# When stores, weight loads and head values are asked for, and how far the filling may run, in a fused attention and recurrence block

## The chip, the cores and the metric

The kernel runs on one core of one Trainium2 chip. The metric is the device time of one execution in microseconds (us), as the median of several runs. The profile is one further execution, taken by the hardware profiler. In it TensorE is PE, its weight loads PEld, VectorE DVE, ScalarE ACT, GpSimd POOL and SyncE SP.

## The reference

One residual block over 1024 rows of width 1024, in float32. Two branches work on the same normalised input: stick-breaking attention with 8 heads of 64, and a gated linear recurrence (HGRN2) with 4 heads of 128. Each branch is projected, gated, and the sum is projected again; a feed-forward part follows.

```python
xn = rmsnorm(x, norm1_g)
q_sb, k_sb, v_sb, f_raw, i_hg, q_hg, g_hg, gate_sb, gate_hg = split(xn @ w_in)
o_sb = merge(stick_breaking_attention(q_sb, k_sb, v_sb))       # 8 heads
o_hg = merge(rmsnorm(hgrn2_chunkwise(silu(q_hg), (1 - lb) * sigmoid(-f_raw), i_hg, log_f)))
o_hg = o_hg * silu(g_hg)                                        # 4 heads
merged = sigmoid(gate_sb + b) * (o_sb @ w_o_sb) + sigmoid(gate_hg + b) * (o_hg @ w_o_hg)
h = x + merged @ w_out
return h + square(relu(rmsnorm(h) @ w_ff1)) @ w_ff2
```

## The kernel before

Every float32 product is made of three products of parts: each operand is split into a high part (a CAST on ACT) and a low part (a subtraction on DVE), `hi_lo` with its two lines 154 and 159, and `three` issues high by high, low by high and high by low on PE (line 131). A product of 128 rows by 512 columns is one such matmul. Some products are formed with fewer multiplications from sums of blocks (seven products for a 2 by 2 arrangement), which is why sums of inputs and sums of weights are needed.

The program is one stream of code. A scheduler then places the instructions on each engine by their dependences, costs and due times; the order of the code sets due times, not places. DMAs are issued from three queues, each in order: SP (loads), POOL (stores of intermediate tiles and some loads from DRAM) and ACT (a few stores).

The parts that matter here, in order of time:

- **Input sums (early_sums, about 59 to 72 us).** From the transposed input four sums are formed for each of two column blocks (forms 6, 5, 7, 3), split into `efh` and `efl`, and each of the 16 tiles (512 KB each) is stored on POOL's queue to `form..` for the gates' projections, which load them again (`gsh`, `gsl`) at about 557 to 598 us. `vrows` are stores of the attention's values on the same queue, released by ACT's copies `v<-pjv` (line 663).
- **The pairs (ProjPair, about 70 to 165 us).** Four pairs of column blocks of the input projection, each with seven products m1 to m7. `wp1a` and `wp1b` are the raw weights of the second pair (two loads of 256 KB each, on SP's queue, in pieces of 64 columns); `whia` and `wloa` are the split parts of the first. `pu` is a copy on ACT of a product out of the result banks (`ppX`), which frees the bank for the next product: m7 waits for the copy of m6.
- **The attention heads (about 165 to 510 us).** Items of one head and one block of rows: scores `z`, `rm` (a scan on DVE, line 982), transposes `pw`, weights `wTh`, `wTl`, and products `po`. Between them stand filling products, `pga`, `pgq` (the raw gates, RawUnit; `wga0r` are the weights of the first, `wga0t` a split sum of them) and `pji` (values of the recurrence, with weights `wi0`).
- **The recurrence (about 510 to 637 us).** Heads h = 0 to 3, each with levels of decayed scores `sl` (k, q and pp updated on DVE in between), state sums `pk` and `pkv` (the latter with the head's values `v`, loaded from `irows` on POOL's queue by `i_load`), outputs `pho`, their norm (`hon`, ACT and POOL and DVE) and a transpose `pot`. The loop runs over h = 0 to 4; in turn h it works on the levels of head h and the tail of head h - 1. Filling products stand between, at most up to a job that is set for each turn: `j_raw[cb]` is the raw gate of column block cb (`pga`, `pgq`), `j_sb[n]` the n-th block of the attention's output projection (`pys`, with weights `wo00` to `wo03`).
- **The gates (from 637 us).** `gX` is the first of their products; its weights are `wg0`, split into `whig`, `wlog`, `tgh`, `tgl`, and `woh`, `wol`; the next ones are `wg4`.

The loop of the recurrence reads:

```python
FILL = (3.6, 3.1, 2.65, 2.45, 2.8)
for h in range(NHG + 1):
    lev = hg_levels(h) if h < NHG else iter(())
    tail = hg_tail(h - 1) if h > 0 else iter(())
    upto = (j_hg[2], j_hg[3], j_raw[6], j_sb[1], j_sb[3])[h]
    if h > 0:
        i_load(h - 1)
    ...
                owed += FILL[h]
                st.advance(int(owed), upto)
```

Of the kernel before, what the change touches and what calls it, by code (L numbers as in the profile page):

```python
# [9 lines left out]
F32 = mybir.dt.float32  # L10
# [9 lines left out]
P = 128  # L20
# [8 lines left out]
NHG = 4  # L29
# [10 lines left out]
def kernel(  # L40
# [19 lines left out]
    nc = tc.nc  # L60
# [11 lines left out]
    wpool = ctx.enter_context(tc.tile_pool(name="wts", bufs=2))  # L72
    psum = ctx.enter_context(tc.tile_pool(name="psum", bufs=8, space=PSUM))

    def slot(name, dt=F32):
        return spool.tile([P, 1024], dt, tag="s", name=name)
# [11 lines left out]
    def dram(name, shape):  # L88
        return scratch.tile(shape, F32, tag=name, name=name)
# [4 lines left out]
    def bank(name):  # L94
        return psum.tile([P, 512], F32, tag="p", name=name)
# [66 lines left out]
    def hi_lo(h, l, src):  # L162
        hi_copy(h, src)
        return lo_sub(l, src, h)
# [518 lines left out]
    def v_split(h):  # L683
        r = vraw.pop(h)
        nc.vector.tensor_tensor(out=r[:, 0:512], in0=r[:, 512:], in1=r[:, 0:512], op=ALU.subtract)
        vt[h] = slot(f"V{h}", F32R)
        V = vt[h].rearrange("p (t s d) -> p t s d", s=2, d=DHS)
        hi_lo(V[:, :, 0, :], V[:, :, 1, :], r[:, 0:512].rearrange("p (t d) -> p t d", d=DHS))
# [90 lines left out]
    def early_whole(half_, engine):  # L779
        for kp in range(KT // 2):  # L780
            h, l = (t.bitcast(F32) for t in xn.t[half_, kp])
            early[half_, kp // 2, kp % 2] = t = slot(f"xw{half_}{kp}")
            engine.tensor_tensor(out=t, in0=h, in1=l, op=ALU.add)

    early_forms = {}
    formd = {(m, kp): dram(f"form{m}{kp}", [P, 2, T]) for m in (3, 5, 6, 7) for kp in range(2)}

    def early_sums():
        def form(m, kp, src):
            early_forms[m, kp] = tuple(slot(f"ef{n}{m}{kp}", F32R) for n in "hl")  # L790
            hi_lo(*early_forms[m, kp], src)
            for i, t in enumerate(early_forms[m, kp]):
                nc.gpsimd.dma_start(formd[m, kp][:, i, :], t.bitcast(F32))

        w = early

        def tt(out, a, b, op):
            nc.vector.tensor_tensor(out=out, in0=a, in1=b, op=op)

        for kp in range(2):  # L800
            tt(w[1, 1, kp], w[1, 0, kp], w[1, 1, kp], ALU.add)
            tt(w[1, 0, kp], w[0, 0, kp], w[1, 0, kp], ALU.subtract)
            tt(w[0, 0, kp], w[1, 1, kp], w[0, 0, kp], ALU.subtract)
            form(6, kp, w[0, 0, kp])
        for kp in range(2):
            form(5, kp, w[1, 1, kp])
        for kp in range(2):
            form(7, kp, w[1, 0, kp])
        for kp in range(2):
            tt(w[0, 1, kp], w[0, 1, kp], w[0, 0, kp], ALU.subtract)  # L810
            form(3, kp, w[0, 1, kp])

    class ProjPair:
# [6 lines left out]
        def load(self):  # L820
            self.raw = []
            for n, parts in (("a", self.pa), ("b", self.pb)):
                r = wpool.tile([P, 1024], F32, tag="raw", name=f"wp{self.i}{n}")
                c = 0
                for c0, w in parts:
                    load(
                        r.rearrange("p (k c) -> p k c", k=KT)[:, :, c : c + w],
                        W_IN[:, c0 : c0 + w].rearrange("(k p) c -> p k c", p=P),
                    )
                    c += w  # L830
                self.raw.append(r)
# [106 lines left out]
    def scores(h, qb):  # L938
        open_block("main")
        nk = (qb + 1) * P  # L940
        QH, QL, KS = qk[h]
        rm = slot_n(f"rm{h}_{qb}", nk)
        step = 320 if nk == 640 else 512
        for s0 in range(0, nk, step):
            m = min(nk - s0, step)
            n = max(m, 256)
            z = bank(f"z{h}_{qb}_{s0}")
            for i, Q in enumerate((QH, QL)):
                matmul(
                    z[:, :n],  # L950
                    Q[:, qb * P : (qb + 1) * P],
                    KS[:, s0 : s0 + n],
                    start=i == 0,
                    stop=i == 1,
                )
            nc.scalar.activation(rm[:, s0 : s0 + m], z[:, :m], AF.Sigmoid, scale=-0.125)  # L956
        zs[h, qb] = rm
# [14 lines left out]
    def weights(h, qb):  # L972

        nk = (qb + 1) * P
        rm = zs[h, qb]
        cut = qb == NT - 1
        parts = ((512, nk), (0, 512)) if cut else ((0, nk),)
        for i, (a, b) in enumerate(parts):  # L980
            rr = rm[:, a:b][:, ::-1]
            sc = nc.vector.tensor_tensor_scan(  # L982
                out=rr,
                data0=rr,
                data1=bits[:, 1024 - nk + a : 1024 - nk + b][:, ::-1],
                initial=rm[:, b : b + 1] if i else 0.0,
                op0=ALU.mult,
                op1=ALU.max,
            )
            if i == 1 or (qb == 5 and h in (2,)):  # L990
                after(sc, turn_lo[0])
# [134 lines left out]
    def i_load(h):  # L1126
        hg[h, "v"] = slot(f"v{h}")
        nc.gpsimd.dma_start(
            chunks(hg[h, "v"]),
            irows[:, h * P : (h + 1) * P].rearrange("(t p) c -> p t c", p=P),  # L1130
        )
# [9 lines left out]
    j_hg = {}  # L1141
# [327 lines left out]
    raw_units = [RawUnit(cb) for cb in range(KT)]  # L1469

    def raw_job(cb):
        u = raw_units[cb]

        def steps_of(ps, wt, w0, half_, k0, start):
            wh, wl = u.hl[wt]
            for k in range(4):
                c = (w0 + k) * P
                xh, xl = xn.mov(k0 + k, half_)
                three(
                    ps, wh[:, c : c + P], wl[:, c : c + P], xh, xl, start and k == 0, k == 3, True  # L1480
                )
                if k % 2 == 1:
                    yield

        def body():
            p1, p14, g1 = (half(f"{n}_{cb}") for n in ("p1", "p14", "g1"))
            ps, p4 = bank(f"pga{cb}"), bank(f"pgq{cb}")
            if cb >= 6:
                load_g1(cb - 6)
            if cb >= 4:  # L1490
                osb[cb - 4] = slot(f"osr{cb - 4}")
                load(osb[cb - 4], osd[cb - 4])
            yield from steps_of(ps, 0, 0, 0, 0, True)
            hi_behind[0] = nc.scalar.copy(p1, ps)
            nc.scalar.dma_start(pd[cb][:, 0, :], p1)
            if cb == 0:
                u.split_t()
            st.prefetch()
            hi_behind[0] = None
            yield from steps_of(p4, 1, 0, 1, 4, True)  # L1500
            add(p14, p1, p4)
            nc.gpsimd.dma_start(pd[cb][:, 1, :], p14)
            yield from steps_of(ps, 0, 4, 0, 4, False)
            nc.scalar.activation(g1, ps, AF.Sigmoid, bias=gate_bias(0, cb))
            nc.scalar.dma_start(gd[cb], g1)
            if cb >= 4:
                a_sb.put(cb - 4, osb[cb - 4])

        return st.add([u], body)
# [55 lines left out]
    j_raw = [raw_job(0)]  # L1565
# [11 lines left out]
    j_sb = [sb_job(cp) for cp in range(4)]  # L1577
# [740 lines left out]
    proj = [ProjPair(i, *blocks[2 * i : 2 * i + 2]) for i in range(4)]  # L2318
# [3 lines left out]
    proj[0].split_plain()  # L2322
    proj[0].m1()
    proj[0].split_sums()
    for o, n in zip(proj, proj[1:] + [None]):
        o.m2()
        if n:
            n.load()
        else:
            scores(*items[0])  # L2330
        o.m6()
        if not n:
            weights(*items[0])
        o.m5()
        if n:
            n.split_plain()
        else:
            scores(*items[1])
        if o is proj[-2]:
            qk_load(0)  # L2340
            v_load(0)
        o.m7()
        if n:
            n.m1()
            n.split_sums()
        o.m4()
        o.m3()
    v_split(0)

    n_fill = 4 * 7 + 2 * 9 + 2 * 17  # L2350
# [4 lines left out]
    for i, it in enumerate(items):  # L2355
# [19 lines left out]
        r = turn(*it, between)  # L2375
# [14 lines left out]
    for h in range(NHG + 1):  # L2390
        lev = hg_levels(h) if h < NHG else iter(())
        tail = hg_tail(h - 1) if h > 0 else iter(())
        upto = (j_hg[2], j_hg[3], j_raw[6], j_sb[1], j_sb[3])[h]
        if h > 0:
            i_load(h - 1)
        if h == 1:
            hg[0, "g"] = slot("g0")
            nc.gpsimd.dma_start(hg[0, "g"], gsd)
        going = True
        while going:  # L2400
            going = False
            for g in (lev, tail):
                if next(g, StopIteration) is not StopIteration:
                    going = True
                    owed += FILL[h]
                    st.advance(int(owed), upto)
                    owed -= int(owed)
        if h + 1 < NHG:
            st.finish(j_hg[h + 1])
        if h > 1:  # L2410
            a_hg.put(h - 2, ohg[h - 2], hg_level[0])
# [102 lines left out]
```

## Time and profile before

| | us |
|---|---|
| runs before: median (lowest to highest of 3) | 1481.63 (1476.57 to 1483.03) |
| the profiled execution | 1478.12 |
| its span, first to last instruction | 1476.4 |
| TensorE busy in it | 1434.8 (97%) |
| DVE, ACT, POOL busy | 1085.1 (73%), 648.9 (44%), 175.8 (12%) |
| mean granted TensorE clock | 0.990 |

The span is 1.7 us shorter than the profiled execution's own time, which is 3.5 us under the median of the runs. A wait is read from the profile as the idle time of an engine ahead of an instruction, with what ended it in brackets. The granted clock (PEclk) is 1.00 at full speed.

### The profile page before, as it was taken

The page shows a single profiled execution, that of the slowest core. Times are in us where ns is not written, and L with a number is a line of the kernel's source. Part 1 is how long each engine was busy: PE and PEld are TensorE (multiplying, and loading weights), DVE is VectorE, ACT ScalarE, POOL GpSimd, SP SyncE. Part 2 cuts the span into 40 slices and gives each one's busy share as a digit, 9 for nine tenths or more (in the row PEclk, how much of TensorE's full clock was granted, in tenths as well). Part 3 has the DMA queues.
Part 4 walks back from the last instruction along what each step waited for, and adds up shares of the span by engine and source line. Part 5 has one row for each costly group of instructions (what it writes and reads, how often), then busy time and mean ns, then how long its engine had stood idle before and what let it go on. Part 6 is the DMA issues. An engine that isn't in the chain of part 4 may idle for free. (4 is left out here: it accounts for less than half of the span.)

```text
span 1476.4 us, 19878 instructions
## 1 busy us (share of the span) xinstructions
PE 1434.8 (97%) x7422; PEld 1220.5 (83%) x7422; DVE 1085.1 (73%) x1526; ACT 648.9 (44%) x1056; POOL 175.8 (12%) x333
## 2 busy tenths in 40 slices
PE   8979899999999999799998999999999999999998
PEld 8968799988888888688887888888888888888886
DVE  6946688798976888568875899676766666768765
ACT  6433566566322333333333575444444443433433
POOL 3322222322000011101110110000000000000032
PEclk9999999999999999999999999999999999999999
DMA  6576765986211267655468533444444985676835
GB/s 222 183 222 206 228 175 161 216 178 152 72 44 44 67 212 277 216 167 175 143 197 262 199 127 129 157 157 156 154 145 151 341 294 199 228 270 235 290 102 187
DMA packets 170857, 270.82 MB, mean 183 GB/s; under 512 B 27612, under 2 KB 95752, under 8 KB 170760
## 3 DMA queue, kind: packets, MB, share of 16 engines
q1 hardware_dynamic: 149272, 206.36, 42.6%
q0 software_dynamic: 17744, 56.64, 12.3%
q10 hardware_dynamic: 3744, 6.56, 1.2%
q8 instruction: 58, 0.95, 0.3%
q14 instruction: 39, 0.32, 0.1%
HBM read 192.44 MB, written 85.46 MB: 188 GB/s over the span
## 5 line engine op out<-in xcount | busy, mean ns | idle before, releaser
L154 ACT CAST whid<-w 128x1024 fp32r<-128x1024 f32 x30 | 31.6, 1053 | 153.6 <-PE pm L131 86.0
L982 DVE TENSOR_TENSOR_SCAN rm<-rm,bits 128x512 f32<-128x512 f32 (+6 forms) x72 | 87.4, 1222 | 8.9 <-ACT rm L956 8.4
L131 PE MATMUL pm<-wlod,sh 128*128 128x512 f32 x240 | 93.5, 389 | 0.0
L131 PE MATMUL pm<-whid,sh 128*128 128x512 f32 x240 | 93.4, 389 | 0.0
L131 PE MATMUL pm<-whid,sl 128*128 128x512 f32 x240 | 93.4, 389 | 0.0
L131 PE MATMUL pm<-tl,sh 128*128 128x512 f32 (+1 forms) x210 | 81.3, 387 | 0.0
L131 PE MATMUL pm<-th,sl 128*128 128x512 f32 (+1 forms) x210 | 81.3, 387 | 0.0
L131 PE MATMUL pm<-th,sh 128*128 128x512 f32 (+1 forms) x210 | 81.3, 387 | 0.0
L159 DVE TENSOR_TENSOR wlod<-w,whid 128x1024 fp32r<-128x1024 f32 x30 | 36.7, 1223 | 59.0 <-ACT whid L154 58.7
L2123 POOL TENSOR_SCALAR fss<-fss 128x1 f32<-128x1 f32 x8 | 4.5, 562 | 562.1 <-ACT fsc L2118 561.6
L159 DVE TENSOR_TENSOR sl<-sa,sh 128x1024 fp32r<-128x1024 f32 x56 | 68.2, 1218 | 1.0 <-ACT sh L154 1.0
L1030 ACT ACTIVATE wTh<-pw,minus_one 128x512 fp32r<-128x512 f32 (+2 forms) x96 | 53.4, 583 | 33.1 <-PE pw L134 29.1
L1036 DVE SCALAR_TENSOR_TENSOR wTl<-pw,wTh 128x512 fp32r<-128x512 f32 (+2 forms) x96 | 50.4, 548 | 16.3 <-ACT wTh L1030 15.6
L154 ACT CAST sh<-sa 128x1024 fp32r<-128x1024 f32 x56 | 57.2, 1045 | 7.0 <-DMA sa<-ad 7.0
L131 PEld LDWEIGHTS pm<-wlod,sh 128*128 128x128 f32 x240 | 45.0, 187 | 9.9 <-DVE wlod L159 0.6
L131 PEld LDWEIGHTS pm<-whid,sl 128*128 128x128 f32 x240 | 45.1, 188 | 9.4
L131 PEld LDWEIGHTS pm<-whid,sh 128*128 128x128 f32 x240 | 45.1, 188 | 9.2
L131 PE MATMUL pX<-sql,t1h 128*128 128x512 f32 x128 | 50.0, 391 | 0.1
L131 PE MATMUL pX<-sqh,t1l 128*128 128x512 f32 x128 | 49.8, 389 | 0.0
L131 PE MATMUL pX<-sqh,t1h 128*128 128x512 f32 x128 | 49.8, 389 | 0.0
L131 PEld LDWEIGHTS pm<-tl,sh 128*128 128x128 f32 x210 | 39.5, 188 | 8.2
L131 PEld LDWEIGHTS pm<-th,sh 128*128 128x128 f32 x210 | 39.4, 188 | 8.0
(962 smaller groups left out, 4573.5 us busy)
## 6 DMA issues: line engine op xcount, KB each, us to landing
w<-in_w_ff_dram SPq DMA_DIRECT2D x72, 512.0 KB, 5.4
sa<-ad SPq DMA_DIRECT2D x56, 512.0 KB, 6.5
ad<-a SPq DMA_DIRECT2D x32, 256.0 KB, 4.4
ad<-s SPq DMA_DIRECT2D x16, 512.0 KB, 5.6
tw<-in_w_out_dram POOLq DMA_DIRECT2D x24, 256.0 KB, 6.0
x<-in_x_dram SPq DMA_DIRECT2D x8, 512.0 KB, 8.4
qkh<-qkh POOLq DMA_DIRECT2D x16, 256.0 KB, 3.9
qkl<-qkl POOLq DMA_DIRECT2D x16, 256.0 KB, 4.7
```

The lines of the kernel that those rows point to most:

```text
L131: return pe(nc.tensor.matmul(*a, **k))
L154: hi_last[0] = after(in_turn("act", nc.scalar.copy(dst, src)), hi_behind[0])
L159: nc.vector.tensor_tensor(out=dst, in0=src, in1=hi.bitcast(F32), op=ALU.subtract),
L982: sc = nc.vector.tensor_tensor_scan(out=rr, data0=rr, data1=bits[:, 1024 - nk + a : 1024 - nk + b][:, ::-1], initial=rm[:, b : b + 1] if i ...
L1030: nc.scalar.activation(th[:, 0:n, qs], src, AF.Identity, bias=minus_one),
L1036: nc.vector.scalar_tensor_tensor(out=tl[:, 0:n, qs], in0=src, scalar=-1.0, in1=th[:, 0:n, qs].bitcast(F32), op0=ALU.add, op1=ALU.subtract,),
L2123: nc.gpsimd.tensor_scalar(out=ssq, in0=ssq, scalar1=1.0 / D, scalar2=EPS, op0=ALU.mult, op1=ALU.add)
```

## The change

It has four edits, in code order:

1. `early_sums` no longer issues the 16 stores itself. It puts them on a list (`kept`), and `keep(n)` issues the next n of them on POOL's queue. Over the last three pairs `spread` asks for one store at each of seven places; what is left is issued after the pairs.
2. The raw weights of the second pair go into slots of their own and not into the two buffers that the pairs share; they are loaded ahead of the pairs' loop, and each turn of the loop then loads the weights of the pair after the next.
3. The first raw gate's weights are loaded ahead of `weights(*items[0])`, and split (with the split sum `wga0t`) in the last pair, ahead of m4. Until now `wga0t` was split inside the gate's own job.
4. In the recurrence `i_load(h)` stands in turn h (was: `i_load(h - 1)`), and the filling may run to `j_raw[7]` in turn 2 and `j_sb[2]` in turn 3 (was `j_raw[6]`, `j_sb[1]`).

```diff
+    kept = deque()
+
+    def keep(n):
+        for _ in range(min(n, len(kept))):
+            dst, t = kept.popleft()
+            nc.gpsimd.dma_start(dst, t.bitcast(F32))
...
-            for i, t in enumerate(early_forms[m, kp]):
-                nc.gpsimd.dma_start(formd[m, kp][:, i, :], t.bitcast(F32))
+            kept.extend((formd[m, kp][:, i, :], t) for i, t in enumerate(early_forms[m, kp]))
...
-                r = wpool.tile([P, 1024], F32, tag="raw", name=f"wp{self.i}{n}")
+                if self.i == 1:
+                    r = slot(f"wp{self.i}{n}")
+                else:
+                    r = wpool.tile([P, 1024], F32, tag="raw", name=f"wp{self.i}{n}")
...
-            if cb == 0:
-                u.split_t()
...
-    for o, n in zip(proj, proj[1:] + [None]):
+    proj[1].load()
+    for o, n, m in zip(proj, proj[1:] + [None], proj[2:] + [None] * 2):
+        def spread():
+            if o is not proj[0]:
+                keep(1)
+
         o.m2()
-        if n:
-            n.load()
-        else:
+        if m:
+            m.load()
+        elif not n:
             scores(*items[0])
+        spread()
         o.m6()
         if not n:
+            raw_units[0].load()
             weights(*items[0])
+        spread()
...
         o.m7()
+        spread()
         if n:
             n.m1()
             n.split_sums()
+        else:
+            raw_units[0].split()
+            raw_units[0].split_t()
+        spread()
         o.m4()
+        spread()
         o.m3()
+    keep(len(kept))
     v_split(0)
...
-        upto = (j_hg[2], j_hg[3], j_raw[6], j_sb[1], j_sb[3])[h]
-        if h > 0:
-            i_load(h - 1)
+        upto = (j_hg[2], j_hg[3], j_raw[7], j_sb[2], j_sb[3])[h]
+        if h < NHG:
+            i_load(h)
```

What this does to the order on the engines is seen at four places. First ACT around m6 and m7 of the first pair. `pu<-ppX` of line 890 is the copy of m1's product, 899 that of m6 and 908 that of m7 (899, 908 and 917 in the changed kernel, whose lines stand nine further on here); `whia_1155` and `whia_1145` are the second pair's. Before:

```order
68 L154 CAST whib_1094<-wp0b 128x1024
69 L890 COPY pu_1084<-ppX_1071 128x512
70 L154 CAST w54h_1098<-wp0a 128x1024
71 L154 CAST qkh_0_1117<-pv_1115 128x512
72 L154 CAST whia_1155<-wp1a 128x1024
73 L899 COPY pu_1084<-ppX_1071 128x512
74 L908 COPY pu_1171<-ppX_1071 128x512
```

and in the changed kernel:

```order
68 L154 CAST whib_1078<-wp0b 128x1024
69 L899 COPY pu_1068<-ppX_1055 128x512
70 L154 CAST w54h_1082<-wp0a 128x1024
71 L154 CAST qkh_0_1107<-pv_1105 128x512
72 L908 COPY pu_1068<-ppX_1055 128x512
73 L154 CAST whia_1145<-wp1a 128x1024
74 L917 COPY pu_1161<-ppX_1055 128x512
```

The copy of m6 moved ahead of the CAST that needs `wp1a`. SP's queue has the same order in both; the load of `wp1a` waits for DVE's `wlob` of the first pair before, and for DVE's last `efl` now.

Second, POOL's queue at the stores of the sums (`form_115` to `form_122` are the eight tensors in DRAM). Before, the 16 stores stand in a row, and here is their end:

```order
56 L793 DMA form_115<-efh_818 128x1024
57 L793 DMA form_115<-efl_819 128x1024
58 L793 DMA form_116<-efh_825 128x1024
59 L793 DMA form_116<-efl_826 128x1024
60 L666 DMA vrows<-v_1_924 128x2x256
61 L666 DMA vrows<-v_2_978 128x2x256
62 L666 DMA vrows<-v_3_1032 128x2x256
63 L705 DMA qkh_101<-qkh_0_1117 128x512
```

In the changed kernel the three stores to `vrows` stand between them, and four of the sixteen behind the first `qkh`, `qkl` of the pairs:

```order
51 L666 DMA vrows<-v_2_962 128x2x256
52 L790 DMA form_118<-efh_793 128x1024
53 L790 DMA form_118<-efl_794 128x1024
54 L790 DMA form_121<-efh_797 128x1024
55 L666 DMA vrows<-v_3_1016 128x2x256
56 L790 DMA form_121<-efl_798 128x1024
57 L790 DMA form_122<-efh_801 128x1024
58 L790 DMA form_122<-efl_802 128x1024
59 L705 DMA qkh_101<-qkh_0_1107 128x512
60 L705 DMA qkl_102<-qkl_0_1108 128x512
61 L790 DMA form_115<-efh_806 128x1024
```

Third, ACT in the first attention item, where the raw gate's split was. Before:

```order
126 L154 CAST wga0t<-wga0r_1692 128x512
127 L1030 ACTIVATE wTh_3_0_1711<-pw_6_0_1798,minus_one 128x4x128
128 L1030 ACTIVATE wTh_3_4_1713<-pw_6_1_1805,minus_one 128x3x128
129 L956 ACTIVATE rm_2_1812<-z_2_0_1813 128x384
130 L154 CAST wi0h_1778<-wi0r_1774 128x1024
131 L1030 ACTIVATE wTh_0_0_1742<-pw_1_0_1835,minus_one 128x2x128
132 L154 CAST wi0h_1782<-wi0r_1776 128x1024
```

In the changed kernel `wga0t` stands at row 110, 16 places earlier, and the two casts `wi0h` behind the first gate's sigmoid `g_0`:

```order
134 L965 ACTIVATE rm_3_1903<-z_3_0_1904 128x512
135 L1511 ACTIVATE g_0_1705<-pga_1706,prm 128x512
136 L1512 DMA gd_143<-g_0_1705 128x512
137 L154 CAST wi0h_1778<-wi0r_1774 128x1024
138 L154 CAST wi0h_1782<-wi0r_1776 128x1024
139 L965 ACTIVATE rm_4_1863<-z_4_0_1864 128x320
140 L965 ACTIVATE rm_4_1863<-z_4_320_1868 128x320
141 L1039 ACTIVATE wTh_2_0_1878<-pw_5_0_1882,minus_one 128x4x128
142 L154 CAST wga1whi<-wga1r_1786 128x1024
```

`wga1r` (the second gate's weights) is loaded into buffers that DVE's `wi0l` has to leave first, in both kernels.

Fourth, PE at the end of the recurrence, where `pho_1` and `pot_0`, `pot_1` are the last head's output and its transposes. Before, 12 products `pys` stand between `pho_1` and `pot_0`, and 18 between `pot_0` and `pot_1` and again between `pot_1` and `gX`:

```order
2951 L131 MATMUL pys_0_6393<-asbl_5861,wo03h_6253 128x512
2952 L131 MATMUL pys_0_6393<-asbh_5860,wo03l_6254 128x512
2953 L134 MATMUL pot_0_6406<-ident,hon_0_6323 128x128 x4
2954 L131 MATMUL pys_1_6414<-asbh_5485,wo03h_6253 128x512
2955 L131 MATMUL pys_1_6414<-asbl_5486,wo03h_6253 128x512
```

In the changed kernel nothing does:

```order
2987 L131 MATMUL pho_1_6436<-k_5100,q_5216 128x128
2988 L134 MATMUL pot_0_6455<-ident,hon_0_6402 128x128 x4
2989 L134 MATMUL pot_1_6461<-ident,hon_1_6438 128x128 x4
2990 L131 MATMUL gX_6482<-gsh_5949,whig_6258 128x512
2991 L131 MATMUL gX_6482<-gsl_5950,whig_6258 128x512
```

The products moved into the recurrence's turns 2 and 3: 12 `pga` and 12 `pgq` now stand between `pot_1` and `sl_6` at the end of turn 2, and 12 `pys` ahead of `pot_1` at the end of turn 3; there `pot_1`, `sl_5`, `sl_6` and `pk` still follow one another without filling. From `gX` on PE's order is the same in both.

More of the change, by code (lines that the diff above doesn't have):

```diff
@@ L2345 @@
             n.split_sums()
+        else:
+            raw_units[0].split()
+            raw_units[0].split_t()
+        spread()
         o.m4()
+        spread()
         o.m3()
+    keep(len(kept))
     v_split(0)
```

## The prediction

> **What bounds the kernel now.** I read the page's first part, then PE's waits, then the stretches in which those waits lie. One row of the page settles which engine counts:
>
> ```profile
> PE 1434.8 (97%) x7422; PEld 1220.5 (83%) x7422; DVE 1085.1 (73%) x1526; ACT 648.9 (44%) x1056; POOL 175.8 (12%) x333
> ```
>
> PE is busy for all but 41.6 us of the span of 1476.4. The change removes no matmul and adds none, so it can only act on PE's idle time and on what PE does slowly after it. PE's list of waits says where the idle time is (columns: the waiting group and what it waited for; us in all, times, longest):
>
> ```profile
> PE ppX L131 <- ACT pu L899: 7.6, 1, 7.6
> PE pkv L131 <- DMA v<-irows: 4.9, 1, 4.9
> PE sl L131 <- DVE pp L167: 4.6, 3, 2.0
> PE pwW L131 <- DVE h L1401: 4.2, 1, 4.2
> PE pji L131 <- DVE wTl L1036: 2.8, 1, 2.8
> PE pgq L131 <- ACT wga0t L154: 1.4, 1, 1.4
> PE pgq L131 <- DVE wga0t L159: 1.1, 1, 1.1
> ```
>
> All but `pwW`, which the change does not touch, lie where it moves something: 22.4 us. A wait costs more than its length, since the granted clock falls with it. In the table by stretches I read PE's busy us (third column) and the PEclk:
>
> ```profile
> 90.00:95.00 5.00, 1.27 (x3) 1.08 (x4) 1.74 (x2) 1.53 (x2) 0.00 (x0) 0.59 0.57 128
> 95.00:100.00 5.00, 5.00 (x17) 3.94 (x17) 1.56 (x3) 0.60 (x2) 0.00 (x0) 0.72 0.00 0
> 185.00:190.00 5.00, 3.84 (x19) 3.84 (x20) 5.00 (x8) 4.11 (x9) 0.00 (x0) 0.66 0.40 138
> 545.00:550.00 5.00, 3.10 (x27) 2.40 (x25) 4.12 (x13) 1.18 (x3) 1.30 (x2) 0.83 1.03 370
> 550.00:555.00 5.00, 5.00 (x23) 4.08 (x22) 4.29 (x8) 2.00 (x4) 0.00 (x0) 0.83 0.11 38
> 600.00:605.00 5.00, 5.00 (x25) 4.29 (x24) 3.08 (x9) 3.39 (x5) 0.00 (x0) 0.71 0.98 363
> 610.00:615.00 5.00, 1.95 (x9) 1.98 (x10) 0.00 (x0) 0.00 (x0) 0.00 (x0) 0.82 0.88 284
> 615.00:620.00 5.00, 5.00 (x27) 4.41 (x27) 3.87 (x9) 0.00 (x0) 0.00 (x0) 0.84 0.02 6
> ```
>
> I count busy time times (1 - PEclk) as lost: 0.52 + 1.40 = 1.9 us after the gap of 7.6; 1.3 after the 2.8; 0.53 + 0.85 = 1.4 at 545 to 555; 1.45 at 600 to 605; 0.35 + 0.80 = 1.15 after the 4.9. So the places cost: pairs 9.5; first gate 1.4 + 1.1 = 2.5 and `pji` 4.1, together 6.6; end of turn 2, turn 3 and the values, below, 13.7.
>
> **Second pair's weights (9.5 us at stake).** On ACT and PE:
>
> ```profile
> 92.15 1.04 ACT L154 CAST whia<-wp1a 128x1024 fp32r<-128x1024 f32 x1 [10.00 <-DMA wp1a<-in_w_in_dram]
> 93.10 0.58 ACT L899 COPY pu<-ppX 128x512 f32<-128x512 f32 x1
> 93.73 0.79 PE L131 MATMUL ppX<-efh,whib 128*128 128x512 f32 x1 [7.56 <-ACT pu L899]
> 98.45 0.39 PE L131 MATMUL ppX<-xnh,whia 128*128 128x512 f32 x1
> ```
>
> m7 waited for a short copy that stood behind a CAST that waited for a load. Now the copy stands ahead, so m7 waits for nothing; the gap is gone if m1 finds `whia` and `wloa`. PE will be at m1 at about 98.45 - 9.7 = 88.7 (9.7 being the 7.56, the 1.9 and 0.2 of issue); with 1.0 for the CAST and 1.2 for DVE's part the load must be in by about 86.4. When it lands hangs on the stores. SP's issue, and the queues' rows of packets and MB (q0 is POOL's stores, q1 SP's loads): both queues in the stretch 82 to 84 us, q1 in 88 to 90, both in 90 to 92.
>
> ```profile
> 77.91 1.95 SPq L139 DMA_DIRECT2D wp1a<-in_w_in_dram  x2
> q0 software_dynamic: 197, 0.71, 88.5%
> q1 hardware_dynamic: 136, 0.03, 7.6%
> q1 hardware_dynamic: 613, 0.15, 34.1%
> q1 hardware_dynamic: 1494, 0.38, 83.1%
> q0 software_dynamic: 2, 0.00, 1.0%
> ```
>
> `wp1a`'s 512 KB are some 2,000 packets of about 250 B. The first of them passed after 82, 4 us behind the issue; beside the stores they went at 68 to 306 per us, alone at 747; all were in at 92.15, when the stores had drained. The change asks at about 71.7, and stores are paced by ACT's copies:
>
> ```profile
> 69.78 0.38 ACT L663 COPY v<-pjv 128x256 f32<-128x256 f32 x1
> 75.30 0.37 ACT L663 COPY v<-pjv 128x256 f32<-128x256 f32 x1 [1.98 <-PE pjv L131]
> 81.53 0.62 ACT L154 CAST qkh<-pv 128x512 fp32r<-128x512 f32 x1 [1.89 <-DVE pv L883]
> ```
>
> Four stores of together 1.8 MB go out after 69.8, four after 75.3, the last after 82; at some 0.37 MB per us (0.71 + 0.03 in 2 us) each batch takes 4.9 us and ends about when the next begins, the second at about 80.4. If nothing passes till 75.7, the slow rates give `wp1a` some 300 to 1,500 packets by 80.4, and alone the rest takes 0.7 to 2.3 us; with up to 3 us for a last slow piece it lands between 82 and 86. I take 9.0 of the 9.5 (bounds 2, rival 2 below, and 9.5). That the stores are not spread over three pairs costs nothing by itself: they still end before the loads of `gsh` at 557.
>
> The Trainium skill, "DMA: Bandwidth & Descriptors", section "Queues, rings and completion order", says that a DMA engine takes turns between its queues, and a turn is a whole packet of some 9 to 17 descriptors. As an estimate from that page and the rows, 13 of `wp1a`'s 128 pieces per engine against 13 store pieces of 3.6 KB at 23 GB/s is 2.0 us a turn and 10 turns, about 20 us: landing at 92 after all, were the stores unbroken. The trace agrees with the slow rate (136 in 2 us is 4 per engine and us, and 13 per 2 us is 6.5).
>
> **First raw gate (6.6 at stake).** `wga0t` is split before it is needed, so the 2.5 us go. But the two casts `wi0h` now stand behind the gate's sigmoid, and behind them DVE's `wi0l`, the load of `wga1r` into the buffers that it leaves, and ACT's `wga1whi`:
>
> ```profile
> 174.43 1.06 ACT L154 CAST wi0h<-wi0r 128x1024 fp32r<-128x1024 f32 x1
> 177.49 2.25 SPq L139 DMA_DIRECT2D wga1r<-in_w_in_dram  x2
> 183.20 1.04 ACT L154 CAST wga1whi<-wga1r 128x1024 fp32r<-128x1024 f32 x1 [3.45 <-DMA wga1r<-in_w_in_dram]
> ```
>
> Followed by hand in the clock of before: with PE 2.5 earlier the sigmoid stands at about 179.6 (PE's scores ahead of it, not ACT, set that), the casts with their rows' 1.05 each end at 182.3 and the split after them lets the load out at about 182.7, that is 5.2 later than 177.49; with the 5.7 us that it took (183.20 - 177.49), `wga1whi` starts at 188.4. Behind it on ACT stand the `wTh` and `rm` of the next blocks, for which PE's `pw` and `po` wait. They come out between 0.3 us earlier and 1.1 later than before. So the wait moves and is not removed: I take -0.4 us (a loss), with bounds of +6.6 (nothing waits) and -3 (a load of 9 us as in the stores' burst).
>
> **Recurrence (13.7 at stake).** Its waits one by one:
>
> ```profile
> 547.14 0.65 PE L131 MATMUL sl<-q,k 128*64 128x64 f32 x8 [1.90 <-DVE pp L167]
> 595.39 1.37 PE L131 MATMUL sl<-q,k 128*32 128x32 f32 x32 [0.71 <-DVE pp L167]
> 598.79 1.75 PE L131 MATMUL sl<-q,k 128*64 128x64 f32 x16 [2.04 <-DVE pp L167]
> 606.41 0.54 POOL L1556 DMA_DIRECT2D yd<-g1r  x1 [15.59 <-DVE g1r L167]
> 606.94 0.92 POOL L1128 DMA_DIRECT2D v<-irows  x1
> 613.05 1.31 PE L131 MATMUL pkv<-v,pp 128*128 128x128 f32 x5 [4.94 <-DMA v<-irows]
> ```
>
> - Values: `v<-irows` stood on POOL behind a store that waited for DVE till 606.41. In the changed order it stands some 50 us earlier, behind `pd` of the last raw gate. The 4.9 + 1.15 = 6.1 go.
> - Turn 2: 24 gate products (5.4 us at 0.227 each) now cover the wait of 1.90; 1.9 + 1.4 = 3.3 go.
> - Turn 3: 12 `pys` ahead of `pot_1` cover the 0.71, but not the 2.04 between `sl_5` and `sl_6`. DVE's splits of `wg0` and `wo` now stand there too, some 2.4 us. Of 0.71 + 2.04 + 1.45 + 0.1 = 4.3 I leave 3.5 (bounds 1.5 and 6).
> - The end: nothing stands between `pho_1`, `pot_0`, `pot_1` and `gX`, so `pot_1` waits for the norm:
>
> ```profile
> 625.46 0.28 ACT L1355 ACTIVATE hon<-pho 128x128 f32<-128x128 f32 x1 [0.53 <-PE pho L131]
> 628.02 0.69 DVE L167 TENSOR_TENSOR hon<-pho,hn_y 128x512 f32<-128x512 f32 x1 [2.11 <-POOL hn_y L253]
> ```
>
> From the end of `pho_1` (0.3 before 625.46) to 628.71 is 3.6 us; `pot_0` fills 0.35. A new wait of 3.25 and, as after the 2.8, a slow tail of 1.5: 4.8 (bounds 3 and 10, rival 3).
>
> 13.7 - 3.5 - 4.8 = 5.4 saved. Everything from `gX` on keeps its order and shifts along.
>
> **Sum.** 9.0 - 0.4 + 5.4 = 14.0 off the profiled 1478.1 gives 1464.1. That execution is 3.5 under the median, inside a spread of 6.5; against the median the same sum gives 1467.6. I forecast 1466. Half a per cent (7.4 us) is about what a measurement of this kernel can tell from no change.
>
> **The rivals.**
> 1. The first gate's section keeps its gain, because the load of `wga1r` is quick or PE has other work: 6.6 + 0.4 more, 1459. For it: PE has `pji` products there that need the casts alone. Against: the 5.7 us of the rows above, with 5.2 us of delay ahead of them.
> 2. The spreading does not do what it says: the stores still fill the DMA engines till 90, and `wp1a` lands at 92 as before. m7 is free, but m1 waits from 88.7 to about 94.4 with a tail of 1.9: 2 saved and not 9, 1473. For it: 12 of 16 stores still go out before 78.
> 3. Splits of `wg0` and `wg4` ahead of the chain on in-order engines: ACT's cast of `wg4` now stands ahead of `hon`'s squares, so a late load delays `pot_1`. If it were issued at 625.94 as before, 10 us instead of 3.25: 1473.
> 4. Slower: the same `wg4` subtractions on DVE stand ahead of the copy of `pkv` that `pho_0` needs. The load goes out some 5 us before DVE is there and `pho_0` needs it about 10 us after its issue; from there on every us costs PE one. To end above 1489 it must take about 10 + 14 + 7 = 31 us. For it, the DMA engines are at 0.98 at 600 to 605; against it, the longest landing in any row above is 14.2 (`wp1a`), in the stores' burst.
>
> **How the numbers follow.** Forecast (1461 to 1471) 0.56; rival 1, 0.10; rival 2, 0.13; rival 3, 0.13; nothing gained, both 2 and 3, 0.04; rival 4, 0.04. The range goes from rival 1 less 3 to rivals 2 and 3 plus 3: 1456 to 1476. Faster than 1474.2: 0.56 + 0.10 + about three fifths of 0.26 = 0.82; same 0.14; slower 0.04.
>
> **What would show it.** Right would be: no wait of `ppX` on `pu`; `wp1a` landing by 86; no wait of `pgq` on `wga0t`, but a new one of `pji`, `pw` or `po` near 175 to 195; no wait of `pkv` on `v`; one of `pot` on `hon` of about 3 us ahead of `gX`. The forecast is wrong if the gate's section shows no wait (faster), if m1 waits for `wloa`, or if `pho` or `pot` waits for a load's split.

## The result and the profile after

The changed kernel takes 1460.57 us (median of 4 runs, 1458.68 to 1464.32) against 1482.33 us (4 runs, 1476.57 to 1483.07): a ratio of 0.9865, 95% interval 0.9833 to 0.9897. On a second chip, in five rounds: 1461.98 (6 runs, 1460.9 to 1468.31) against 1479.29 (9 runs, 1478.8 to 1485.3), 0.987 (0.9851 to 0.9889). The forecast was 1466, between 1456 and 1476, and faster. The profiled execution of the changed kernel took 1464.32 us with a span of 1462.6; it is the highest of its four, while that of the kernel before (1478.12) lies below three of its own four. So the two traces differ by 13.8 and the medians by 21.8.

The engines in the page after, and PE's waits after (columns as before: us in all, times, longest):

```profile
PE 1431.0 (98%) x7422; PEld 1215.5 (83%) x7422; DVE 1084.5 (74%) x1526; ACT 648.6 (44%) x1056; POOL 176.2 (12%) x333
```

```profile
PE pwW L131 <- DVE h L1410: 5.2, 1, 5.2
PE po L131 <- DVE wTl L1045: 3.6, 5, 1.1
PE pot L134 <- DVE hon L167: 2.9, 1, 2.9
PE sl L131 <- DVE q L167: 2.8, 2, 2.3
...
PE pji L131 <- ACT rm L965: 2.0, 1, 2.0
PE pw L134 <- DVE rm L991: 1.5, 1, 1.5
PE po L131 <- ACT rm L965: 1.1, 1, 1.1
```

Gone are the 7.6 of `ppX`, the 4.9 of `pkv` and the 2.5 of `pgq`. The rows of `pot`, `pji`, `pw` and the second `po` are new, and `sl` keeps waits of 2.8 in all, the longest 2.3 (2.0 before), for `q` now. PE's busy time is 3.8 us less with the same 7422 matmuls: fewer of them ran in a slow tail, the stretch at a lowered granted clock behind a wait.

The table by stretches shows where the clock fell this time (PE's busy us in the third column, PEclk behind the engines):

```profile
90.00:95.00 5.00, 5.00 (x24) 4.14 (x23) 3.80 (x6) 3.81 (x6) 1.09 (x2) 1.00 1.06 391
170.00:175.00 5.00, 2.88 (x15) 1.93 (x16) 3.57 (x5) 4.41 (x7) 0.00 (x0) 1.00 0.56 150
595.00:600.00 5.00, 2.66 (x21) 2.10 (x20) 5.00 (x14) 0.96 (x2) 0.54 (x1) 0.91 0.74 230
600.00:605.00 5.00, 5.00 (x19) 4.00 (x18) 2.83 (x6) 1.91 (x3) 0.39 (x1) 0.75 0.18 52
615.00:620.00 5.00, 2.22 (x20) 1.98 (x19) 1.92 (x3) 2.48 (x10) 1.20 (x2) 0.96 0.66 248
620.00:625.00 5.00, 4.84 (x18) 4.07 (x19) 2.15 (x4) 2.52 (x3) 0.00 (x0) 0.70 0.01 3
```

In these stretches two tails are left, at 595 to 605 (turn 3's `sl`) and at 615 to 625 (`pot`). The second pair (90 to 95) runs full. In the first attention item (170 to 175) PE is 58% busy and keeps the whole clock.

I divide both traces by the first start of a PE group: of `ppX<-efh` (pair 0), of `pga` (end of the pairs), of the first product with `wga1whi` (first item), of that with `wga4whi`, of `pyh` (recurrence done), of `pwW`, and of `pm` (end stage). Us between them:

```
                        before    after   difference   forecast
start to ppX<-efh        80.57    80.02      -0.55
to pga      (pairs)      82.66    74.18      -8.48       -9.0
to wga1whi  (gate)       67.97    68.06      +0.09       +0.4
to wga4whi              277.04   276.83      -0.21
to pyh      (recurrence)136.99   131.09      -5.90       -5.4
to pwW                  123.12   122.99      -0.13
to pm                   395.53   396.87      +1.34
```

Up to `pyh` the trace gained 15.05; 1.2 were lost behind it, where the order is the same. Among all kernels here the last row lies between 393.5 and 396.9, so it is scatter.

### The profile page after: what moved, and what is told of

It is laid out like the page before. It is cut to its first block, busy times and chain, and to the rows that moved or that the text cites. A ratio compares the mean times of both kernels' runs of the same rounds, so it can differ in the third digit from the quotient of the medians.

```text
span 1462.6 us, 19885 instructions
## 1 busy us (share of the span) xinstructions
PE 1431.0 (98%) x7422; PEld 1215.5 (83%) x7422; DVE 1084.5 (74%) x1526; ACT 648.6 (44%) x1056; POOL 176.2 (12%) x333
## 5 line engine op out<-in xcount | busy, mean ns | idle before, releaser
L1039 ACT ACTIVATE wTh<-pw,minus_one 128x512 fp32r<-128x512 f32 (+3 forms) x96 | 53.4, 582 | 32.1 <-PE pw L134 28.0
L1045 DVE SCALAR_TENSOR_TENSOR wTl<-pw,wTh 128x128 fp32r<-128x128 f32 (+3 forms) x96 | 50.3, 546 | 19.3 <-ACT wTh L1039 16.6
L131 PEld LDWEIGHTS pm<-th,sl 128*128 128x128 f32 x210 | 39.5, 188 | 8.0
```

The source lines that it names most:

```text
L131: return pe(nc.tensor.matmul(*a, **k))
L1039: nc.scalar.activation(th[:, 0:n, qs], src, AF.Identity, bias=minus_one),
L1045: nc.vector.scalar_tensor_tensor(out=tl[:, 0:n, qs], in0=src, scalar=-1.0, in1=th[:, 0:n, qs].bitcast(F32), op0=ALU.add, op1=ALU.subtract,),
```

## The experiments

Each takes the changed kernel and undoes or adds one thing (two in the last pair). The times are of one run where nothing else is said; what decides is the trace: the section, and which instruction waits in it. For scale, the kernel before took 1484.1 on the chip of the first four experiments and 1479.29 on that of the next four.

**1. Stores issued at once again.**

```diff
-            kept.extend((formd[m, kp][:, i, :], t) for i, t in enumerate(early_forms[m, kp]))
+            for i, t in enumerate(early_forms[m, kp]):
+                nc.gpsimd.dma_start(formd[m, kp][:, i, :], t.bitcast(F32))
```

> The changed kernel with the 16 stores of the sums issued at once again, as before; all else as changed. Read by the start of the first pga product, which closes the pairs (163.2 us before, 154.2 after). Theory (the stores' burst decides when the second pair's weights land): wp1a is asked for at 71 but gets a few per cent of the DMA engines until the stores have drained at about 90, so it lands at 90 to 92; m7 does not wait, its copy being ahead on ACT, but m1 waits from about 88 to 94: pga at 160 to 162, the profiled time some 6 to 8 us above the changed kernel's 1464. Rival (asking early in buffers of its own is what counts): wp1a lands by 86, pga at 154 to 155, no difference.

1471.77; pairs 80.22 us. PE's wait, and ACT's cast in the timeline of this kernel:

```profile
PE ppX L131 <- ACT whia L154: 3.8, 1, 3.8
```

```profile
91.54 1.04 ACT L154 CAST whia<-wp1a 128x1024 fp32r<-128x1024 f32 x1 [7.49 <-DMA wp1a<-in_w_in_dram]
```

Asked for early but beside unbroken stores, `wp1a` came at 91.5, as late as in the kernel before (92.15), and m1 waited: this is rival 2 of the prediction, and 6.0 of the 8.5 us are gone with the spreading.

**2. The second pair's weights asked for as before.**

```diff
-                if self.i == 1:
-                    r = slot(f"wp{self.i}{n}")
-                else:
-                    r = wpool.tile(...)
+                r = wpool.tile(...)
...
-    proj[1].load()
...
-        if m:
-            m.load()
-        elif not n:
+        if n:
+            n.load()
+        else:
```

> The changed kernel with the second pair's weights loaded as before (in the pairs' two buffers, asked for at about 78 and not 71); stores stay interleaved. On ACT the cast of wp1a is again ahead of the copy of m6. Theory (the stores' burst decides): the second batch of stores has drained at about 80, so wp1a passes from about 80 on and lands at 82 to 87; m7 waits 0 to 3 us: first pga at 154 to 158. Rival (the early asking counts): the wait of 7.6 us comes back, pga at 163.

1466.59; pairs 79.18 us. Neither 154 to 158 nor 163: `pga` started at 160.39.

```profile
87.87 1.04 ACT L154 CAST whia<-wp1a 128x1024 fp32r<-128x1024 f32 x1 [5.08 <-DMA wp1a<-in_w_in_dram]
```

With the stores spread the load issued at 78.56 is in by 87.9, 4 us sooner than before, but the copy stands behind the cast again and m7 waits 2.6 for it. Either edit without the other gains 2.4 and 3.5 us of the section, both together 8.5. The length alone would not show this: the changed kernel's own pairs once took 79.50 us (experiment 9). What shows it is that here m1 or m7 waits for the late `wp1a`, and there neither does.

Why the pair works is seen in the queues. Rows of the DMA queues (packets, MB; q0 the stores, q1 the loads) of the changed kernel at 74 to 76 and 76 to 78 us:

```profile
q0 software_dynamic: 112, 0.42, 77.0%
q1 hardware_dynamic: 205, 0.05, 11.4%
q1 hardware_dynamic: 1693, 0.43, 99.8%
q0 software_dynamic: 44, 0.16, 27.2%
```

and of experiment 1 at 76 to 78:

```profile
q0 software_dynamic: 201, 0.73, 91.0%
q1 hardware_dynamic: 176, 0.05, 9.9%
```

In the changed kernel the stores pause at 76 to 78 and q1 moves 1693 packets, eight times those of the stretch before: with 141 at 72 to 74 that makes 2039, as many as nearly all of the 2048 pieces of `wp1a`. Without the spreading there is no pause at 76 to 78.

**3. The first gate's split back in its old place.**

```diff
+            if cb == 0:
+                u.split_t()
             st.prefetch()
...
-            raw_units[0].load()
...
-        else:
-            raw_units[0].split()
-            raw_units[0].split_t()
```

> The changed kernel with the first raw gate loaded and split as before. Read by the time from the first pga product to the first product with the second gate's weights wga1whi (68.0 us before, 68.1 after). Theory (the edit only moves the wait, since the casts wi0h move behind the gate's sigmoid): the waits of pgq for wga0t (2.5 us) and of pji for wTl (2.8) come back and the waits of pji, pw and po at 173 to 185 go; 68.0 again, total time the same within 1 us. Rival (the edit gains its 2.5 us and something else lost them): 70 to 71.

1462.56; first item 67.91 us against 68.06. Its waits:

```profile
PE pji L131 <- DVE wTl L1045: 2.7, 1, 2.7
...
PE pgq L131 <- ACT wga0t L154: 1.4, 1, 1.4
PE pgq L131 <- DVE wga0t L159: 1.1, 1, 1.1
```

The old waits are back, `pw`'s and the new `po`'s are gone, and the section is as long as with the edit. This edit only moves a wait.

**4. The first item's weight casts ahead of the attention's next block.** They stood behind the gate's sigmoid; an order edge puts them ahead.

```diff
-            hi_behind[0] = None
+            hi_behind[0] = hi_last[0] if cb == 0 else None
```

> The changed kernel with an order edge that puts ACT's next wTh after the two casts wi0h, so that these stand ahead of the first item's weights again, and the load of wga1r goes out earlier. Theory (the late casts hold the load of wga1r and what stands behind its cast): the waits of PE at 173 to 185 (7.5 us in all) shrink to 1 to 4; from the first pga to wga1whi 62 to 66 us and not 68.1, the profiled time 2 to 6 us below the changed kernel's. Rival (the first item's chain of scan, transposes and weights on DVE and ACT is what limits there): 67.5 to 68.5, other names in PE's list of waits.

1466.4; the section grew to 70.04 us. ACT's timeline in this kernel:

```profile
165.99 1.05 ACT L154 CAST wi0h<-wi0r 128x1024 fp32r<-128x1024 f32 x1 [3.34 <-DMA wi0r<-in_w_in_dram]
168.79 1.52 ACT L1039 ACTIVATE wTh<-pw,minus_one 128x512 fp32r<-128x512 f32 x3
```

```profile
PE po L131 <- ACT wTh L1039: 3.0, 1, 3.0
```

Now ACT itself stood 3.3 us before a cast whose load was not in (and 0.8 before the next), and the `wTh` behind them were late. My theory that the late casts hold the section fell in this form, and the rival's 67.5 to 68.5 is missed too: with the casts some 5 us earlier it got longer. `wga1r` was asked for at 168.32 and not 173.93, but its cast stands at 175.43, only 2.6 us sooner. Whether it could be shorter with a sooner load of `wi0r` was not tried.

**5 and 6. The values asked for late again (caps raised); the caps as before (values early).**

```diff
-        if h < NHG:
-            i_load(h)
+        if h > 0:
+            i_load(h - 1)
```

> The changed kernel with the head values asked for one turn later again (i_load(h - 1)), caps as changed. Read by the start of the first gX product less the start of the first wga4whi product, that is the recurrence (128.8 us before, 121.8 after). Theory (the load of the last head's values stands behind a store that waits for DVE): PE waits some 4 to 6 us for the values again, with a slow tail: 126 to 128.5. Rival (with more filling in turn 3 the store ahead of the load is released in time): 121.5 to 123.

```diff
-        upto = (j_hg[2], j_hg[3], j_raw[7], j_sb[2], j_sb[3])[h]
+        upto = (j_hg[2], j_hg[3], j_raw[6], j_sb[1], j_sb[3])[h]
```

> The changed kernel with the caps of the filling as before (j_raw[6], j_sb[1]), values asked for early as changed. From the first wga4whi product to the first gX (128.8 before, 121.8 after). Theory (the higher caps only move the waits, and the gain of the recurrence is all the values'): the waits of sl for pp at the ends of turns 2 and 3 come back (1.9, 0.7 and 2.0 with their slow tails, 6.8 in all by the trace of before), and the wait of pot for hon (2.9 with its tail 4.4, a part of it behind gX) and of sl for q (5.1 with its tail) go: 120 to 122, and to the first pyh product 1 to 3 us less than the changed kernel's. Rival (the caps gain by themselves): 124 to 126.

The late values: 1460.6, from `wga4whi` to `gX` 121.32 us (before 128.83, changed 121.84), and PE does not wait for `v` at all. The load in POOL's timeline, and the product that needs it in PE's:

```profile
597.38 0.92 POOL L1137 DMA_DIRECT2D v<-irows  x1 [0.39 <-issue]
```

```profile
604.71 1.72 PE L131 MATMUL pkv<-v,pp 128*128 128x128 f32 x14
```

My theory fell here and the rival's size held, but not because the load goes out sooner. Counted from `wga4whi` (499.16 here, 508.24 before) it is issued at 98.2, and at 98.7 before (606.94). What moved is PE: it wants `pkv` at 105.6, before at 99.9 (613.05 less the 4.94 of waiting). With the raised caps PE comes to `pkv` 5.7 us later, which covers the 4.9.

With the old caps and early values: 1463.08, to `gX` 122.92, to `pyh` 131.08 (changed 131.09). PE's waits:

```profile
PE sl L131 <- DVE pp L167: 5.6, 3, 2.8
...
PE gX L131 <- DVE gu L1407: 1.3, 1, 1.3
```

The three old waits of `sl` are there (4.6 before, 5.6 now) and no wait of `pot`. The theory's 120 to 122 and its 1 to 3 us less to `pyh` are both missed, and so is the rival's 124 to 126: the waits of `sl` that came back are as long as the waits that went (5.6 against 5.8 in the recurrence of the changed kernel). So each edit alone gives the recurrence's whole gain. With the caps the filling goes ahead of `pkv` and is missing at `pot`; with the early values it isn't needed there and stays for the end.

**7 and 8. Less filling late, so that some is left for the end.** `FILL` is the filling per step of a turn; the last entry is the last turn.

```diff
-    FILL = (3.6, 3.1, 2.65, 2.45, 2.8)
+    FILL = (3.6, 3.1, 2.65, 2.45, 1.4)
```

> The changed kernel with half the filling per step in the last turn (FILL[4] 1.4 and not 2.8), so that 24 of the products stand around pot at its end. From the first wga4whi to the first pyh product (131.1 after). Theory (pot waits for hon because nothing stands between): the wait of 2.9 and its slow tail of 1.5 go, at most 1.5 come back at pkv or pho, which have less ahead of them: 127 to 129. Rival (the products only move, and pkv or pho waits as long): 130.5 to 131.5.

1458.16; to `pyh` 126.65 us. The section is 4.4 us shorter: the wait of `pot` is gone with its tail; of `sl` the 2.8 stay.

```diff
-    FILL = (3.6, 3.1, 2.65, 2.45, 2.8)
+    FILL = (3.6, 3.1, 2.65, 2.0, 1.8)
```

> The changed kernel with less filling per step in the last two turns (FILL[3] 2.0 and not 2.45, FILL[4] 1.8 and not 2.8): 12 products stand ahead of sl_5 and 12 ahead of sl_6 in turn 3, and 12 and 6 around pot at the end. From the first wga4whi to the first pyh product (131.1 after). Theory: the wait of sl (2.8 with a tail of 2) and that of pot (2.9 with a tail of 1.5) go, at most 2 come back at sl_1 to sl_4, pkv or pho: 122 to 125. Rival (DVE's chain through the levels limits turn 3, and the wait only comes earlier): 126 to 129.

1459.23; to `pyh` 128.19, in the rival's range. Filling kept back in turn 3 too: `sl` no longer waits, but PE reaches the next product that the same chain feeds:

```profile
PE pkv L131 <- ACT pp L1325: 3.9, 1, 3.9
```

In this trace the filling moved the wait along the chain and did not take it away: PE was ahead of DVE and ACT.

**9. The changed kernel again, five rounds.**

> The changed kernel once more, with more runs beside the kernel before. Theory (what the trace of the profiled pair shows, 13.8 us, is all there is): 0.989 to 0.992 of the time before. Rival (the runs' medians, 1460.57 against 1482.33, are nearer the truth than the profiled pair): 0.984 to 0.988.

The times stand at the top: 0.987 is in the rival's range, so the pair of traces shows less than the runs do. The profiled execution was the longest, 1468.31, and its trace shows where: a wait that the first trace of this kernel does not have, and a tail behind it.

```profile
PE ppY L131 <- DVE pv L892: 3.5, 1, 3.5
```

```profile
95.90 0.69 DVE L861 TENSOR_TENSOR wp1a<-wp1b,wp1a 128x512 f32<-128x512 f32 x1 [9.48 <-DMA wp1b<-in_w_in_dram]
```

```profile
95.00:100.00 5.00, 2.03 (x5) 1.65 (x6) 3.34 (x6) 1.62 (x3) 0.96 (x2) 0.72 0.57 131
100.00:105.00 5.00, 5.00 (x16) 3.94 (x15) 4.53 (x6) 2.48 (x3) 0.67 (x2) 0.60 0.36 135
```

DVE stood at the second half of the pair's weights, `wp1b`, with `pv` behind it. 3.5 + 2.03 x 0.28 + 5.00 x 0.40 = 6.1 us, which is about what this execution has over the median. In the trace of the first measurement the same subtraction starts at 88.00. q1 and q0 of the late one at 86 to 88 us, and at 88 to 90:

```profile
q1 hardware_dynamic: 1724, 0.43, 104.1%
q0 software_dynamic: 38, 0.12, 20.4%
q0 software_dynamic: 231, 0.81, 100.6%
q1 hardware_dynamic: 41, 0.01, 2.3%
```

The pause between two batches of stores ended just before the last pieces of `wp1b`: in the three stretches behind it 41, 12 and 42 pieces passed beside the next batch, and the load was in at 95.9. Of the ten traces with these stores and loads, seven have that subtraction at 88.0 to 88.9 and no such wait above 0.2; the other three have it at 92.6, 93.9 and 95.9, with waits of `ppY` of 0.7, 1.8 and 3.5. It is needed by about 92.

**10 and 11. DVE's splits out of the chain, and less filling at the end.** In turn 3 the planner may start `wg0`'s splits (`wlog`, and behind them `wol`) after 8 steps; after 11 they come behind the last level.

```diff
-        yield from range(8)
+        yield from range(11)
...
-    FILL = (3.6, 3.1, 2.65, 2.45, 2.8)
+    FILL = (3.6, 3.1, 2.65, 2.45, 1.4)
```

> As f2_fill (FILL[4] 1.4), and the split of the first gate's weights wg0 set three places later in the filling (range(11) for range(8) ahead of gp[0].split()), so that on DVE wlog and wol stand behind the last level and not between sl_5 and sl_6 of the last head. From the first wga4whi to the first pyh product (131.1 after, 126.7 for f2_fill). Theory (the splits on DVE, 1.14 + 0.6 us, are most of the wait of 2.3 at the second half of sl_6): that wait shrinks to under 1 us and its tail of 2 with it: 122.5 to 125. Rival (DVE's chain is the limit and the wait only comes later, at pkv or pho, or gX waits for the late split): 126 to 128.

1456.78 (4 runs, 1455.81 to 1458.1), ratio 0.9839 (0.9819 to 0.9858) to the kernel before, on the chip of experiment 9; 5.2 under the changed kernel there. To `pyh` 124.64 us. Where the changed kernel had 0.47 and 2.34 (quoted below), this trace has

```profile
594.12 0.65 PE L131 MATMUL sl<-q,k 128*64 128x64 f32 x8 [0.47 <-DVE pp L167]
595.38 0.68 PE L131 MATMUL sl<-q,k 128*64 128x64 f32 x8 [0.61 <-DVE q L167]
```

and from 590 to 620 the granted clock is 1.00 in every stretch. It has the lowest median of the versions that were run. Of the 6.5 us that the section is shorter than in the changed kernel, 4.4 came with the filling (experiment 7 has 126.65) and 2.0 with the later splits; the latter rests on two traces, and 1.7 of it is a tail that experiment 7 has behind its wait of `sl` and this trace has not. The waits of `sl` fell from 2.8 to 1.1.

```diff
-    FILL = (3.6, 3.1, 2.65, 2.45, 2.8)
+    FILL = (3.6, 3.1, 2.65, 2.2, 1.6)
```

(with the same 11 steps)

> As f6_late with FILL[3] 2.2 and FILL[4] 1.6: 12 products stand between pot_1 and sl_5 at the end of turn 3. From the first wga4whi to the first pyh product. Theory: no wait above 1 us from sl_5 to gX: 122 to 124.5. Rival (as in f5_fill, pkv waits for ACT's copy of pk because the chain runs behind): 126 to 129.

1458.45 (4 runs, 1458.01 to 1459.25), 0.985 (0.9831 to 0.9869); to `pyh` 127.70. The theory fell and the size is the rival's, but PE waits at `sl` for `q` (2.9) and not at `pkv`: keeping filling back in turn 3 costs again, 3.1 us here against experiment 10 and 1.5 in experiment 8 against experiment 7.

## Why the prediction was right

**Pairs, 9.0 forecast, 8.5 in the section (9.0 with the start).** Right in size, and the mechanism holds: the copy `pu` stands ahead of the cast and neither waits for a load any more.

```profile
82.94 0.59 ACT L908 COPY pu<-ppX 128x512 f32<-128x512 f32 x1 [1.34 <-PE ppX L131]
83.42 1.05 ACT L154 CAST whia<-wp1a 128x1024 fp32r<-128x1024 f32 x1
```

The step on the landing was wrong in its number: `wp1a` was in at about 78 by the count of pieces, not at 82 to 86. I let the stores run on as in the trace before, with the second batch ending at 80.4; the pause between the batches at 76 to 78 was enough. And a step was missing: I followed `wp1a` to its deadline and not `wp1b`, which follows it on the same queue and depends on the next pause. In three of ten traces it missed that pause, at a cost of up to 6 us. Rival 2 (the stores still fill the engines) is what experiment 1 shows, not what the changed kernel does. The page rule that I set beside it (the Trainium skill, "DMA: Bandwidth & Descriptors", "Queues, rings and completion order") gave, as an estimate, a load at 92 for unbroken stores, at 6.5 pieces per engine and us, which is 104 over the 16. Experiment 1 bears out the rate and not the sum: from 76 to 86 its stretches have 176 to 209 pieces in 2 us, 88 to 104 per us. But none passed from the issue at 71.6 to 76.1, and half of the 2048 passed after 86, as the stores thinned out. That its cast starts at 91.5 is in part luck.

**First gate, -0.4 forecast, -0.1 measured.** The wait moved, as followed by hand. In the trace:

```profile
171.60 1.99 ACT L154 CAST wi0h<-wi0r 128x1024 fp32r<-128x1024 f32 x2 [0.40 <-ACT g L1511]
173.93 1.50 SPq L139 DMA_DIRECT2D wga1r<-in_w_in_dram  x2
178.01 1.05 ACT L154 CAST wga1whi<-wga1r 128x1024 fp32r<-128x1024 f32 x1 [3.18 <-DMA wga1r<-in_w_in_dram]
```

The load took 4.1 us where I took 5.7; shifted by the 9.03 of the pairs the cast stands at 187.0 against the forecast 188.4. Rival 1 (the gain is kept) is out by experiment 3. But experiment 4 shows that my reason is not all of it: with the casts sooner on ACT the section did not shrink, since ACT then stood before them for their own load (3.3 and 0.8 us) and before `wga1whi` for 5.1. What limits this section stays open.

**Recurrence, 5.4 forecast, 5.9 measured.** The sum is right, its attribution is not.
- Values: the wait of `pkv` is gone as forecast, but the early request is not needed for it; the caps alone do it (experiment 5). The step that failed: I set the filling of turns 2 and 3 against the waits of `sl` only, and not against the wait of `pkv` behind them, which it would have covered by itself. By my terms the caps without the early values were worth 3.3 + 0.8 - 4.8 = -0.7; in experiment 5 they are worth 7.4 to `pyh` (136.99 to 129.60), some 6 if a tail behind `pot`, which that trace lacks, is put in (last section).
- Turn 2: its wait is gone, as forecast.
- Turn 3: 3.5 forecast to stay; 0.47 + 2.34 + 2.66 x 0.09 + 5.00 x 0.25 = 4.3 stayed, all that there was before. PE, and DVE between its two waits:

```profile
594.50 0.65 PE L131 MATMUL sl<-q,k 128*64 128x64 f32 x8 [0.47 <-DVE q L167]
597.49 0.68 PE L131 MATMUL sl<-q,k 128*64 128x64 f32 x8 [2.34 <-DVE q L167]
```

```profile
594.26 1.22 DVE L159 TENSOR_TENSOR wlog<-wg0r,whig 128x1024 fp32r<-128x1024 f32 x1
595.40 0.68 DVE L167 TENSOR_TENSOR g1r<-pys,g1r 128x512 f32<-128x512 f32 x1
596.00 0.68 DVE L159 TENSOR_TENSOR wol<-wor,woh 128x512 fp32r<-128x512 f32 x1
```

The 2.4 us of splits and `g1r` (594.26 to 596.68) ahead of the level's products were in the forecast, but I still took 0.8 off for cover, which did not come. Experiment 10 takes the splits out, and the waits of `sl` fall to 1.1.
- End: `pot` waits 2.94, with a tail of 2.22 x 0.04 + 4.84 x 0.30 = 1.5: 4.5 against 4.8. Rivals 3 and 4 are out: neither `pot` nor `pho` waits for a load's split.

By these terms 13.7 - 4.3 - 4.5 = 4.9 was saved, 1.0 less than the 5.9. The 1.0 lies in my tails of before: busy time times (1 - PEclk) over 5 us is too small where the slow part of the 5 us is all busy and the idle part is not slow. The trace of before has three stretches of 3.41 us at 0.50 in the recurrence (from 548.31, 599.51 and 613.16), PE busy in all of them: 5.1 us lost and not 4.1. With waits of 9.6 that makes 14.7; the changed kernel has waits of 5.8 and loses 3.1, together 8.9. The difference is 5.8.

**Sum.** 14.0 forecast and 13.8 between the two traces; part of that closeness is luck, 15.05 won and 1.2 lost in scatter. The median of 1460.57 lies 0.4 below the forecast's inner range (1461 to 1471) and nearer to rival 1's 1459 than to 1466, but rival 1's mechanism is not there: the gate's section gained nothing. Against the medians it is 8 too small on the first chip and 3 on the second (17.3). The 8 is that the profiled execution of the changed kernel lies 3.8 above its median and that of the kernel before 4.2 below. Of the 3.8 some 2.7 can be placed: the first trace of the changed kernel has 74.18 in the pairs and 396.87 in the end stage, where the middle of the other traces is 73.3 (the nine with the same stores and loads) and 395.0 (all twelve). The rest stays open, since only the profiled executions have a trace.

## What to carry to other kernels

Beside a queue full of larger stores the load of many small pieces passed here at about a tenth of the rate that it had in the stores' pauses, so the pauses decided when it landed. So ask before a pause, make one by parting the stores, follow every load up to its own deadline, and check both edits alone, since one without the other may give little. Where two edits each cover the same wait, one by an earlier request and one by work moved ahead of it, count the gain once. And filling moved from one wait to another gains nothing where the chain then makes PE wait at its next product (experiments 8 and 11): take foreign work (here weight splits between two levels on DVE) out of the chain first, then place what filling is left where the last wait is.

## What the runs showed of the hardware

- Pieces of 256 B passed at 68 to 105 per us in the stretches quoted in which a queue of stores (about 3.6 KB a packet) was full, and at about 850 when it paused (205 and 1693 in 2 us, above). The end of a load can be slower still: the last 95 pieces took 6 us, the 1724 ahead of them 2 (experiment 9).
- The tail of the clock does not follow from the wait alone. In the recurrence the granted clock is 1.00 or 0.50, and it falls to 0.50 for 3.41 us, or twice that, at a time (twice in the recurrence of experiments 1, 4 and 9, single elsewhere). The two tails of the changed kernel, taken by these bounds (PE's busy us third, PEclk behind the engines):

```profile
599.09:602.50 3.41, 3.41 (x11) 2.67 (x10) 3.05 (x5) 1.91 (x3) 0.00 (x0) 0.50 0.26 79
619.57:622.98 3.41, 2.82 (x9) 2.44 (x10) 1.29 (x2) 0.88 (x1) 0.00 (x0) 0.50 0.02 5
```

The wait of `pot` is the same in seven of the traces here (2.9 to 3.0). In the changed kernel the second of these stretches begins in it and runs on behind it; in experiment 5 none follows:

```profile
620.00:625.00 5.00, 4.94 (x24) 4.16 (x25) 3.13 (x5) 2.52 (x3) 0.00 (x0) 1.00 0.01 3
```

The recurrence of these seven has the same waits (5.8 us in all) and takes 129.6 to 132.5 us; the time lost at 0.50 goes from 1.7 to 4.7 and makes up this scatter of 2.9. Less its waits and this loss, the recurrence takes 121.9 to 122.9 us in all thirteen traces. So a term for one tail is 0, up to 1.7 or up to 3.4, not 1.5.
- A slow clock can also cost nothing. Waits of 1.99, 1.47 and 1.12 between 173 and 183, where PE was 55 to 71% busy, left the clock at 1.00 in the changed kernel. In experiment 5 the clock was 0.50 from 175.03 to 181.86, behind the same wait of 1.99, and the section from `pga` to `wga1whi` took 67.76 us against 68.06.
